# A hybrid decoder step on one core: paged-cache gathers of eight head dimensions instead of four, with single convolution buffers

## The chip, the core and the metric

The kernel runs on one core of one Trainium2 chip. The metric is the device time of one execution in microseconds. Three runs of the kernel before gave 2805.02, 2815.38 and 2817.81 us, so the median is 2815.38 us.

## What is computed

One layer of an autoregressive decoder, in float32, on 512 prompt tokens and, beside them, on one new token for each of 8 decode sequences. The 520 columns go through the same weights together.

```python
proj = rms_norm(x) @ w_in                 # 2048 -> 7168 + 16
# group A: stick-breaking attention, 8 heads of 128
z  = q.k * SCALE + logit_bias
lb = log_sigmoid(z); l1 = where(valid, lb - z, 0)
a  = where(valid, exp(lb + reverse_cumsum(l1) - l1), 0)
o_sb = rms_norm(a @ v)
# the decode tokens read 2048 cached positions each:
k_past = cache_sb_k[page_table]           # 8 sequences x 16 pages x 128 positions
v_past = cache_sb_v[page_table]
# group B: gated DeltaNet, 8 heads; causal conv of width 4 + SiLU on q, k, v
# then: output projection, residual, gated MLP with a causal conv of width 3,
# a per-layer input gate, final norm
```

## The kernel before, in words

The program is one stream for one core. TensorE does products of 128-row weight tiles with the 520 activation columns, each product as three matmuls on a high and a low part of both operands. A weight tile arrives in `w` by an SP DMA (L238, 512 KB for a half product of eight 128-row blocks), ScalarE casts it to `wh` (L242), and VectorE subtracts to get `wl` (L243). `w` and `wh` have two buffers each, `wl` three (`WB`). One product of `w_in` is two such halves, 96 matmuls of 128x260.

The order of the products is: the per-layer input projection, queries of heads 0 to 3, the eight key convolutions of group B, then four times query, key and value of group A (heads 0 to 3, with the queries of heads 4 to 7), then for the eight heads of group B the q convolution, the v convolution and the gate, then key and value of heads 4 to 7, then the output projection in two parts, and the MLP, whose weights go through a Strassen scheme (`strassen`, `block_product`). Between the products small chains (`sb_chain`, `gdn_chain`, `k_chain`) are advanced step by step by a hand-kept clock (`tick`).

The attention of the decode tokens is laid beside that stream. `decode_k` and `decode_v` read the cache page by page through `gather` (L406 to L411): for one group of four heads and one set of `DC` = 4 head dimensions, four indirect DMAs on the POOL queue, each of 128 rows of `DC` x 128 positions (2 KB a row, 256 KB a gather), fill one `kv` tile of 1 MB. There are two such tiles (`bufs=2`), so a gather for the tile after next waits until VectorE has read the tile before it. VectorE then does `DC` operations of 128x512 on the tile: L436 for keys, L466 for values. With `NDC` = 32 tiles for each of keys and values and two groups of heads there are 128 tiles, 512 gathers and 512 VectorE operations.

The order of instructions on each engine is fixed ahead of time by a planner: it takes ready instructions by priority, with its own estimate of how long each takes. `later(LATE)` puts the decode work last in priority, so it is placed wherever the planner expects an engine to be free and the data to be there. On the chip each engine then works strictly in that order.

```python
def gather(src, g, dc):                                             # L406
    t = dpool.tile([P, 4, DC * PAGE], F32, name="kv", bufs=2)
    for pg in range(4):
        G.indirect_dma_start(out=t[:, pg], out_offset=None, in_=src, in_offset=...)
```

`delta_decode` (L966 to L1044) is the recurrent part for the decode tokens. It needs the q, k and v convolutions of all eight heads. It loads the state in four tiles of 1 MB (`state`, L1000), which take turns in the same two `kv` buffers, and works on each in two pieces of 128x1024: a product (L1014), a reduction (L1016) and an addition (L1018), for two vectors. The value gathers of the second head group stand behind it, but for the first `VSPLIT` = 2 tiles.

`conv` (L594 to L612) copies a finished product to `cb` (ScalarE, L601, L602), writes three zero columns (POOL, L598), scales into `y` (ScalarE, L609) and adds three shifted terms (VectorE, L611 three times). `gdn_conv` then applies SiLU (L625, L626). `cb` and `y` of group B have two buffers each, from the pool `gdn`.

Other parts that the change touches: the tiles `q` and `kT` of an attention head (`sb_head`, two buffers each), the scan in `decode_k` (its result in a tile of its own, L445), the loads `mx` and `xr` ahead of the output projection (L1086, L1101), and the first weights of the MLP: before, a row sum of two weight blocks (`row_sum(0)`, an SP load and an accumulating POOL DMA) is started ahead of `strassen`, and the first block `a11` is loaded to a tile of the pool `wst`.

Of the kernel before, what the change touches and what calls it, by code (L numbers as in the profile page):

```python
# [16 lines left out]
P = 128  # L17
# [14 lines left out]
NPAGE = PAST // PAGE  # L32
DC = 4
NDC = HD // DC
# [6 lines left out]
AFTER = 2  # L41
MXB = 7
KK = 9.0
# [42 lines left out]
def program(tc, i, o):  # L86
# [143 lines left out]
    evacs = []  # L230
    last_wl = [None]
    last_w = [None]

    def weights(src, n, cols=P, after=None, eng=None, pool=None):
        w = wp.tile([P, 8, P], F32, name="w", bufs=WB[0])[:, :n, :cols]
        wh = (pool or wp).tile([P, 8, P], F32R, name="wh", bufs=4 if pool else WB[1])[:, :n, :cols]
        wl = wp.tile([P, 8, P], F32R, name="wl", bufs=WB[2])[:, :n, :cols]
        last_w[0] = nc.sync.dma_start(w, src).ins  # L238
        with contextlib.ExitStack() as st:
            if after is not None:  # L240
                st.enter_context(tc.issue_after(after))
            S.copy(wh, w)  # L242
        last_wl[0] = (eng or V).tensor_tensor(wl, w, wh.bitcast(F32), op=ALU.subtract).ins  # L243
        return wh, wl
# [144 lines left out]
    dpool = pool("dec", 1, "right")  # L389
    gdnp = pool("gdn", 2, "right")  # L390
    tp = gdnp
# [26 lines left out]
    def decode_k(g):  # L418
        with later(-EARLY):
# [6 lines left out]
            S.copy(qd, pq[:, :P])  # L426
        a2 = [dpool.tile([P, 4, PAGE], F32, name=f"dacc{j}") for j in range(2)]
        for dc in range(NDC):
# [15 lines left out]
        V.scalar_tensor_tensor(t1, s, 0.0, t1, op0=ALU.max, op1=ALU.add)  # L444
        inc = dpool.tile([P, 8 * PAGE], F32, name="inc", tag="junk")[:, :T]  # L445
        V.tensor_tensor_scan(inc, t1, zero.broadcast_to([P, T]), 0.0, op0=ALU.add, op1=ALU.add)
        pc = pstd("pc")
        PE.matmul(pc[:, :1], lhsT=C("carry"), rhs=inc[:, T - 1:T], start=True, stop=True)
        nb = dpool.tile([P, 1], F32, name="nb")
        V.tensor_scalar(nb, pc[:, :1], -1.0, None, op0=ALU.mult)  # L450
        V.tensor_tensor(s, s, inc, op=ALU.subtract)
        S.activation(s, s, AF.Exp, bias=nb)
# [4 lines left out]
    def decode_v(g, lo=0, hi=NDC):  # L457
# [3 lines left out]
        for dc in range(lo, hi):  # L461
            with later(LATE):
                vt = gather(i["cv"], g, dc)
                for d in range(DC):
                    junk = n4(dpool.tile([P, 8 * PAGE], F32, name="junk")[:, :4 * PAGE])
                    V.scalar_tensor_tensor(junk, vt[:, :, d], 1.0, A, op0=ALU.mult, op1=ALU.mult,  # L466
                                           accum_out=ov[:, dc * DC + d:dc * DC + d + 1])
# [307 lines left out]
    def sb_head(h):  # L775
        until("sb", ("z", h - 1))
        qT = sbp.tile([P, T], F32, name="q", bufs=2)
        nc.sync.dma_start(qT, qd_[h])
        ps = w_in(H + h)
        kT = sbp.tile([P, T], F32, name="kT", bufs=2)  # L780
        evac_nat(ps, kT, ks[:, h])
# [62 lines left out]
    for h in range(4):  # L844
        queries(4 + h, w_in(4 + h), sbp.tile([P, T], F32, name="q", bufs=2))
        sb_head(h)
# [119 lines left out]
    def delta_decode():  # L966
# [8 lines left out]
        V.tensor_tensor(cf[:, 0:2], cf[:, 0:2], sq, op=ALU.mult)  # L975
        rep = dpool.tile([P, 8 * PAGE], F32, name="rep", tag="junk")[:, :3 * P].rearrange("p (a r c) -> p a r c", a=3, r=2)
        V.tensor_copy(rep, cf.unsqueeze(2).broadcast_to([P, 3, 2, 64]))
# [22 lines left out]
        def state(c):  # L1000
            t = dpool.tile([P, 2, 1024], F32, name="st", tag="kv", bufs=2)
            nc.sync.dma_start(t.rearrange("p a c -> p (a c)"), i["rec"][:, c * 2048:c * 2048 + 2048])
            return t

        sqk = dpool.tile([P, 2, 64], F32, name="sqk")
        with later(LATE):
            for c in range(4):
                t = state(c)
                for a in range(2):
                    ch = c * 2 + a  # L1010
                    s3 = t[:, a].rearrange("p (k v) -> p k v", v=64)
                    for w, vecp in enumerate((qp, kp)):
                        tmp = dpool.tile([P, 8 * PAGE], F32, name="gtmp", tag="junk").rearrange("p (k v) -> p k v", k=16)
                        V.tensor_tensor(tmp, s3, vecp[:, 16 * ch:16 * ch + 16].unsqueeze(2).broadcast_to([P, 16, 64]), op=ALU.mult)  # L1014
                        part = sqk[:, w] if ch == 0 else dpool.tile([P, 64], F32, name="dpart")
# [45 lines left out]
    for h in range(4, H):  # L1061
        sb_head(h)
        if h == SBC:
            drain("gdn0", "gdn1")
            close(n=2)
            fpool = pool("res", 1)
            mpool = pool("mix", 1)
            NRES = 9
# [9 lines left out]
    for part in range(2):  # L1078
# [17 lines left out]
        for m in range(KC):  # L1096
# [3 lines left out]
            else:  # L1100
                xr = tp.tile([P, 544], F32, name="xr", tag="yg")[:, :TOK]  # L1101
                nc.sync.dma_start(xr, i["x"][m])
# [65 lines left out]
    close("right")  # L1168
    close(n=2)
    sp_ = pool("wst", 1)  # L1170
# [36 lines left out]

    row_sums = [row_sum(0)]

    def strassen(m, f, c1, c2):  # L1210
        src1, src2 = i["w_gate"][m], i["w_up"][m]
        b, a, c, d = [mp.tile([P, 512], F32, name=n)[:, 0:HALF] for n in ("pb", "pa", "pc", "pd")]
        a11 = raw(src1[:, :NP], "a11", sp_, 2)
        a12 = raw(src1[:, NP:], "w", wp, WB[0])
        s1 = row_sums.pop()
        p1, u2, u3 = [tp.tile([P, HALF], F32, name=n) for n in ("p1", "u2", "u3")]
# [265 lines left out]
```

## Time and profile before

| | |
|---|---|
| median of three runs | 2815.38 us (2805.02 to 2817.81) |
| the profiled execution, its own time | 2811.4 us |
| span of its trace | 2809.6 us |
| mean granted TensorE clock | 0.979 of full speed |
| TensorE busy | 2654.4 us, 94% of the span |
| VectorE busy | 1900.8 us, 68% |
| GpSimd (POOL) busy | 713.9 us, 25%, most of it before 1210 us |

A trace row names the line, the engine, what it writes and what it reads. "Idle before" is the time in which the engine had nothing running ahead of that instruction, and the releaser is what ended it. The chain of waits is followed back from the last instruction: at each step to what released it, or to the instruction ahead of it on its engine. TensorE's granted clock is 1.00 at 2.4 GHz; the other level is 1.2 GHz, so a mean of 0.95 over a stretch is a tenth of it at the lower level.

### The profile page before, as it was taken

How to read it: one execution, taken by the hardware profiler on the slowest of the kernel's cores; microseconds unless marked ns; L12 is line 12 of the kernel's file. 1: busy time of each engine (PE TensorE's matmuls, PEld its weight loads, DVE VectorE, ACT ScalarE, POOL GpSimd, SP SyncE). 2: the span in 40 equal slices, each digit the busy share in tenths (PEclk: the TensorE clock that was granted, in tenths of full speed). 3: DMA queues.
4: the chain of work that ended last, by engine and by line, in shares of the span. 5: the costliest groups of instructions: out<-in, count | busy, mean ns of one | idle time of the engine just before them, and what ended most of it. 6: DMA issues, size and time to landing. Idle time of an engine off the chain costs nothing.

```text
span 2809.6 us, 52566 instructions
## 1 busy us (share of the span) xinstructions
PE 2654.4 (94%) x21329; PEld 2593.8 (92%) x21329; DVE 1900.8 (68%) x3060; ACT 1159.0 (41%) x1936; POOL 713.9 (25%) x773
## 2 busy tenths in 40 slices
PE   8898899998999898979999999999998999999997
PEld 7898788998998788979999999999998999999997
DVE  7487767677779766677878888888885342433545
ACT  5454444333345541554444444444451131323433
POOL 4565556656650566210000000000000000000000
PEclk9999999999999999989999999999999999999998
DMA  5678778767775778675655555555556453433333
GB/s 189 225 251 257 231 225 265 239 213 230 241 240 151 251 235 264 178 214 159 180 155 177 166 178 165 175 168 175 168 163 226 137 155 93 139 95 94 110 114 114
DMA packets 194083, 519.99 MB, mean 185 GB/s; under 512 B 41712, under 2 KB 51824, under 8 KB 193328
## 3 DMA queue, kind: packets, MB, share of 16 engines
q1 hardware_dynamic: 138672, 336.13, 37.4%
q0 software_dynamic: 55168, 180.50, 21.9%
q8 instruction: 167, 2.74, 0.4%
q14 instruction: 76, 0.62, 0.1%
HBM read 463.05 MB, written 49.76 MB: 183 GB/s over the span
## 4 chain that ended last, share of the span: by engine, by line
PE 55%; DMA 16%; DVE 11%; POOL 8%; issue 8%; ACT 2%; DVEq 0%; POOLq 0%; SPq 0%; ACTq 0%
PE mm L264 25%; PE pb L1198 13%; PE pc L1198 8%; POOL kv L409 8%; DMA kv<-in_ck,idx 6%; DMA kv<-in_cv,idx 6%; PE pa L1198 4%; PE pd L1198 4%; DVE dacc L436 2%; DMA acc<-sqt 1%; DVE wl L243 1%; DVE junk L466 1%; DMA out_recs<-st 1%; DVE yg L611 1%; DVE dpart L1016 1%
## 5 line engine op out<-in xcount | busy, mean ns | idle before, releaser
L264 PE MATMUL mm<-ah,wl 128*128 128x260 f32 x4128 | 856.8, 288 | 30.6 <-DVE wl L243 30.4
L264 PE MATMUL mm<-ah,wh 128*128 128x260 f32 x4128 | 860.9, 289 | 17.6 <-ACT wh L242 12.5
L264 PE MATMUL mm<-al,wh 128*128 128x260 f32 x4128 | 854.4, 288 | 3.8 <-DVE al L374 3.3
L264 PEld LDWEIGHTS mm<-ah,wl 128*128 128x128 f32 x4128 | 649.3, 192 | 40.9 <-DVE wl L243 37.3
L264 PEld LDWEIGHTS mm<-ah,wh 128*128 128x128 f32 x4128 | 651.0, 192 | 25.0 <-ACT wh L242 13.5
L264 PEld LDWEIGHTS mm<-al,wh 128*128 128x128 f32 x4128 | 649.0, 192 | 8.8 <-DVE al L374 4.3
L242 ACT CAST wh<-w 128x1024 fp32r<-128x1024 f32 (+4 forms) x289 | 279.7, 968 | 654.7 <-PE mm L264 575.0
L243 DVE TENSOR_TENSOR wl<-w,wh 128x1024 fp32r<-128x1024 f32 (+4 forms) x282 | 315.7, 1120 | 228.4 <-ACT wh L242 223.2
L409 POOL DMA_INDIRECT kv<-in_cv,idx x256 | 283.5, 1107 | 259.0 <-DVE seed L867 74.2
L409 POOL DMA_INDIRECT kv<-in_ck,idx x256 | 293.3, 1146 | 187.0 <-DVE dacc L436 77.9
L1193 ACT CAST wh<-a 128x1024 fp32r<-128x1024 f32 x172 | 181.0, 1052 | 365.4 <-PE pc L1198 188.1
L466 DVE SCALAR_TENSOR_TENSOR junk<-kv,dacc 128x512 f32<-128x512 f32 x256 | 176.9, 691 | 110.0 <-DMA kv<-in_cv,idx 106.3
L436 DVE SCALAR_TENSOR_TENSOR dacc<-kv,qd,dacc 128x512 f32<-128x512 f32 x252 | 178.4, 747 | 101.0 <-DMA kv<-in_ck,idx 101.0
L1194 DVE TENSOR_TENSOR wl<-a,wh 128x1024 fp32r<-128x1024 f32 x172 | 210.1, 1221 | 43.3 <-ACT wh L1193 43.0
L1198 PE MATMUL pb<-ah,wh 128*128 128x260 f32 x774 | 220.7, 285 | 11.5 <-ACT wh L1193 11.5
L1198 PE MATMUL pb<-ah,wl 128*128 128x260 f32 x774 | 221.7, 286 | 5.6 <-DVE wl L1194 5.5
L1198 PE MATMUL pb<-al,wh 128*128 128x260 f32 x774 | 220.2, 284 | 0.0
L1357 POOL TENSOR_TENSOR y<-h,fr 128x260 f32<-128x260 f32 x8 | 6.9, 887 | 689.2 <-DVE fr L1352 689.2
L1198 PEld LDWEIGHTS pb<-ah,wh 128*128 128x128 f32 x774 | 147.3, 190 | 12.0 <-ACT wh L1193 12.0
L1198 PEld LDWEIGHTS pb<-ah,wl 128*128 128x128 f32 x774 | 147.7, 191 | 7.6 <-DVE wl L1194 7.5
L1198 PEld LDWEIGHTS pb<-al,wh 128*128 128x128 f32 x774 | 147.5, 191 | 0.0
L598 POOL MEMSET cbf<- 128x2 f32 x43 | 4.6, 107 | 543.5 <-DVE yf L611 543.3
(437 smaller groups left out, 4735.2 us busy)
## 6 DMA issues: line engine op xcount, KB each, us to landing
w<-in_w_in SPq DMA_DIRECT2D x112, 512.0 KB
a<-in_w_up SPq DMA_DIRECT2D x86, 512.0 KB
w<-in_w_down SPq DMA_DIRECT2D x48, 512.0 KB
w<-in_w_gate SPq DMA_DIRECT2D x43, 512.0 KB
s<-in_w_up SPq DMA_DIRECT2D x43, 512.0 KB
a<-in_w_gate SPq DMA_DIRECT2D x43, 512.0 KB
s<-in_w_up POOLq DMA_DIRECT2D x43, 512.0 KB, 7.7
w<-in_w_pg SPq DMA_DIRECT2D x32, 512.0 KB
```

Source lines behind the costliest of these rows:

```text
L242: S.copy(wh, w)
L243: last_wl[0] = (eng or V).tensor_tensor(wl, w, wh.bitcast(F32), op=ALU.subtract).ins
L264: last_mm[0] = PE.matmul(ps[:, hf, 0:HALF], lhsT=a, rhs=b[:, hf * HALF:(hf + 1) * HALF], start=(first and n == 0), stop=(last and n == 2)).ins
L409: G.indirect_dma_start(out=t[:, pg], out_offset=None, in_=src, in_offset=bass.IndirectOffsetOnAxis(ap=idx[:, g, dc, pg:pg + 1], axis=0))
L436: V.scalar_tensor_tensor(a2[dd % 2], kt[:, :, d], qd[:, dd:dd + 1], a2[dd % 2], op0=ALU.mult, op1=ALU.add)
L466: V.scalar_tensor_tensor(junk, vt[:, :, d], 1.0, A, op0=ALU.mult, op1=ALU.mult, accum_out=ov[:, dc * DC + d:dc * DC + d + 1])
L611: V.scalar_tensor_tensor(y, cb[:, j:j + L], cw[:, j:j + 1], y, op0=ALU.mult, op1=ALU.add)
L1016: V.tensor_reduce(part, tmp.rearrange("p k v -> p v k"), axis=AX.X, op=ALU.add)
L1193: S.copy(wh, w)
L1194: V.tensor_tensor(wl, w, wh.bitcast(F32), op=ALU.subtract)
L1198: last_mm[0] = PE.matmul(ps, lhsT=a[:, k], rhs=b, start=(start and k + n == 0), stop=(k == NP - 1 and n == 2), skip_group_check=not start).ins
L1357: e.tensor_tensor(y[:, j], hres[m + j][:, c], r, op=ALU.mult)
```

## The change

The gathers take eight dimensions at once, so a row is 4 KB, a gather 512 KB and a tile 2 MB; there are 64 tiles and 256 gathers, and still two tiles in the ring. The number and shape of the VectorE operations on the tiles (L436, L466) stay. The state of `delta_decode` comes in two tiles of two 1 MB loads each, worked on in 16 pieces of 128x512 instead of 8 of 128x1024. Besides, `cb` and `y` of group B, `q` and `kT` get one buffer each; `wl` two until the MLP, with every third one of the first four weight tiles in another pool; the second key accumulator shares its place with `junk`; the scan works in place; `mx` loads get six buffers instead of seven; the `xr` loads alternate between two pools with one buffer each. For the MLP the weight pool is opened again with three `wl`, its first block `a11` goes through the `w` ring, and the first row sum is started inside `strassen`, behind the loads of `a11` and `a12`.

```diff
-DC = 4
+DC = 8
-MXB = 7
+MXB = 6
...
+    WL = [2]
+    third = [0]
...
-        wl = wp.tile([P, 8, P], F32R, name="wl", bufs=WB[2])[:, :n, :cols]
+        third[0] = (third[0] + 1) % 3
+        own = pool if pool and third[0] == 0 else wp
+        wl = own.tile([P, 8, P], F32R, name="wl", bufs=WL[0] if own is wp else 1)[:, :n, :cols]
...
-    gdnp = pool("gdn", 2, "right")
+    gdnp = pool("gdn", 1, "right")
...
-        a2 = [dpool.tile([P, 4, PAGE], F32, name=f"dacc{j}") for j in range(2)]
+        a2 = [dpool.tile([P, 4, PAGE], F32, name=f"dacc{j}", tag=("dacc", "junk")[j]) for j in range(2)]
...
-        inc = dpool.tile([P, 8 * PAGE], F32, name="inc", tag="junk")[:, :T]
-        V.tensor_tensor_scan(inc, t1, zero.broadcast_to([P, T]), 0.0, op0=ALU.add, op1=ALU.add)
+        V.tensor_tensor_scan(t1, t1, zero.broadcast_to([P, T]), 0.0, op0=ALU.add, op1=ALU.add)
...
-        qT = sbp.tile([P, T], F32, name="q", bufs=2)
+        qT = sbp.tile([P, T], F32, name="q")
...
-        kT = sbp.tile([P, T], F32, name="kT", bufs=2)
+        kT = sbp.tile([P, T], F32, name="kT")
...
-            t = dpool.tile([P, 2, 1024], F32, name="st", tag="kv", bufs=2)
-            nc.sync.dma_start(t.rearrange("p a c -> p (a c)"), i["rec"][:, c * 2048:c * 2048 + 2048])
+            t = dpool.tile([P, 2, 2048], F32, name="st", tag="kv", bufs=2)
+            for a in range(2):
+                nc.sync.dma_start(t[:, a], i["rec"][:, c * 4096 + a * 2048:c * 4096 + a * 2048 + 2048])
...
-            for c in range(4):
-                t = state(c)
-                for a in range(2):
-                    ch = c * 2 + a
-                    s3 = t[:, a].rearrange("p (k v) -> p k v", v=64)
+            for c in range(2):
+                t = state(c).rearrange("p a c -> p (a c)")
+                for a in range(8):
+                    ch = c * 8 + a
+                    s3 = t[:, 512 * a:512 * a + 512].rearrange("p (k v) -> p k v", v=64)
...
+            xpool = pool("xres", 1)
...
-                xr = tp.tile([P, 544], F32, name="xr", tag="yg")[:, :TOK]
+                xr = (xpool.tile([P, TOK], F32, name="xr") if m % 2 else tp.tile([P, 544], F32, name="xr", tag="yg")[:, :TOK])
...
-    close(n=2)
+    close(n=4)
+    wp = pool("wts2", 1)
+    WL[0] = WB[2]
...
-    row_sums = [row_sum(0)]
+    row_sums = []
...
-        a11 = raw(src1[:, :NP], "a11", sp_, 2)
+        a11 = raw(src1[:, :NP], "a11", sp_, 2) if m else raw(src1[:, :NP], "w", wp, WB[0])
         a12 = raw(src1[:, NP:], "w", wp, WB[0])
-        s1 = row_sums.pop()
+        s1 = row_sums.pop() if m else row_sum(0)
```

## Rows read from the trace of the kernel before

**Rows 1.** The page, block 1: busy us of each engine over the span, its share of the span and its instructions.

```profile
PE 2654.4 (94%) x21329; PEld 2593.8 (92%) x21329; DVE 1900.8 (68%) x3060; ACT 1159.0 (41%) x1936; POOL 713.9 (25%) x773
```

**Rows 2.** Busy time of each engine by stretches of the span, in us from its start: length, busy us and instructions of each engine, granted clock, DMA share, GB/s. Gathers run in the first, second, third and fifth of them; the sixth is the start of the MLP, the seventh a long stretch of products with no gathers.

```profile
100.00:350.00 250.00, 225.74 (x1691) 214.35 (x1690) 187.06 (x385) 114.03 (x208) 148.49 (x136) 0.95 0.75 237
350.00:590.00 240.00, 223.66 (x1813) 209.40 (x1813) 171.07 (x417) 98.07 (x168) 144.87 (x135) 0.96 0.76 238
590.00:840.00 250.00, 227.42 (x1817) 224.01 (x1816) 187.20 (x360) 93.46 (x219) 154.25 (x143) 0.96 0.72 233
840.00:923.00 83.00, 77.35 (x574) 70.80 (x573) 78.52 (x132) 40.70 (x79) 8.16 (x7) 1.00 0.51 147
923.00:1130.00 207.00, 184.26 (x1339) 171.82 (x1338) 141.75 (x338) 83.19 (x125) 121.08 (x114) 0.96 0.78 257
...
1200.00:1250.00 50.00, 36.47 (x258) 35.09 (x257) 34.60 (x49) 23.26 (x35) 6.52 (x9) 0.83 0.75 217
...
2185.00:2740.00 555.00, 555.00 (x4629) 554.88 (x4628) 216.32 (x256) 165.61 (x205) 0.00 (x0) 1.00 0.37 115
```

**Rows 3.** The chain of waits: shares by line over the whole span (first row), and in the stretch from 600 to 700 us (second row).

```profile
PE mm L264 25%; PE pb L1198 13%; PE pc L1198 8%; POOL kv L409 8%; DMA kv<-in_ck,idx 6%; DMA kv<-in_cv,idx 6%; PE pa L1198 4%; PE pd L1198 4%; DVE dacc L436 2%; DMA acc<-sqt 1%; DVE wl L243 1%; DVE junk L466 1%; DMA out_recs<-st 1%; DVE yg L611 1%; DVE dpart L1016 1%
...
by line: DMA kv<-in_ck,idx 33.5%; POOL kv L409 29.9%; issue 20.5%; DVE dacc L436 9.0%; DVE yg L611 5.1%; DVE wl L243 1.1%; DVE zt L957 0.7%; ACT gv L625 0.6%; ACT gq L625 0.6%; DVEq L436 0.2%; ACT cbg L606 0.2%; ACT cs L626 0.2%; POOLq L409
```

**Rows 4.** Who waited for whom over the span: us in total, times, longest us.

```profile
DVE junk L466 <- DMA kv<-in_cv,idx: 106.3, 44, 5.4
DVE dacc L436 <- DMA kv<-in_ck,idx: 101.0, 43, 6.0
...
POOL kv L409 <- DVE dacc L436: 85.4, 26, 14.3
...
POOL kv L409 <- DVE junk L466: 74.1, 31, 6.8
```

**Rows 5.** The gathers (L409): duration in ns (least, median, most), the time from issue to landing, and two gathers in a row on POOL, with the idle time ahead of each.

```profile
L409 POOL DMA_INDIRECT kv<-in_ck,idx x256: 940/960/3297, 81.5 to 811.5; - x128
...
DMA to landing us min/median/max: 3.3/4.9/8.5
...
675.79 0.95 POOL L409 DMA_INDIRECT kv<-in_ck,idx  x1 [1.35 <-DVE dacc L436]
677.04 0.95 POOL L409 DMA_INDIRECT kv<-in_ck,idx  x1 [0.30 <-issue]
```

**Rows 6.** The VectorE operations on the gathered tiles: busy us in all, mean ns of one, idle before.

```profile
L436 DVE SCALAR_TENSOR_TENSOR dacc<-kv,qd,dacc 128x512 f32<-128x512 f32 x252 | 178.4, 747 | 101.0 <-DMA kv<-in_ck,idx 101.0
L466 DVE SCALAR_TENSOR_TENSOR junk<-kv,dacc 128x512 f32<-128x512 f32 x256 | 176.9, 691 | 110.0 <-DMA kv<-in_cv,idx 106.3 <-ACT dacc L452 0.2
```

**Rows 7.** Another DMA that POOL issues, of 512 KB: duration on POOL in ns (least, median, most), and from the page's list of DMA issues its size and the median us from issue to landing.

```profile
L1205 POOL DMA_DIRECT2D s<-in_w_up x43: 866/872/1252, 1210.3 to 2043.7; - x43
...
s<-in_w_up POOLq DMA_DIRECT2D x43, 512.0 KB, 7.7
```

**Rows 8.** ScalarE in order of time, three places in the key convolutions: the evacuation of a product to `cbg` (L601) stands ahead of the SiLU of the convolution before it (L625), which waits for that one's last L611. The last number in brackets is ScalarE's idle time.

```profile
165.56 0.58 ACT L601 COPY cbg<-mm 128x512 f32<-128x512 f32 x1
168.86 0.63 ACT L625 ACTIVATE gk<-yg 128x512 f32<-128x512 f32 x1 [1.35 <-DVE yg L611]
...
180.26 0.57 ACT L601 COPY cbg<-mm 128x512 f32<-128x512 f32 x1
182.15 0.63 ACT L625 ACTIVATE gk<-yg 128x512 f32<-128x512 f32 x1
...
221.65 0.58 ACT L601 COPY cbg<-mm 128x512 f32<-128x512 f32 x1
224.74 0.63 ACT L625 ACTIVATE gk<-yg 128x512 f32<-128x512 f32 x1 [1.13 <-DVE yg L611]
```

**Rows 9.** The work of `delta_decode` on the state, and a product of 128x512 from elsewhere (L1053): duration in ns, first and last start.

```profile
L1014 DVE TENSOR_TENSOR gtmp<-st,qkv x16: 1211/1218/1225, 850.7 to 917.0; 128x1024 f32<-128x1024 f32 x16
...
L1016 DVE TENSOR_REDUCE dpart<-gtmp x14: 1903/1982/2010, 860.8 to 919.5; 128x64 f32<-128x1024 f32 x14
...
L1018 DVE TENSOR_TENSOR sqk<-sqk,dpart x14: 208/216/225, 863.5 to 921.7; 128x64 f32<-128x64 f32 x14
...
L1053 DVE TENSOR_TENSOR up<-kvg,kvg x16: 684/691/694, 2122.3 to 2179.9; 128x512 f32<-128x512 f32 x16
```

**Rows 10.** The cast `wh` (L242): what ended ScalarE's idle time ahead of it, in us and times; and the subtractions `wl` (L243) on VectorE from 100 to 350 us and from 350 to 1130 us (count, busy us, mean ns, idle before).

```profile
  PE mm L264: 575.0, 166
...
  DMA w<-in_w_in: 8.8, 4
...
L243 DVE TENSOR_TENSOR wl<-w,wh 128x1024 fp32r<-128x1024 f32 x31 | 37.8, 1219 | 6.3 <-ACT wh L242 6.3
...
L243 DVE TENSOR_TENSOR wl<-w,wh 128x1024 fp32r<-128x1024 f32 (+1 forms) x100 | 114.5, 1145 | 7.0 <-ACT wh L242 6.7
```

**Rows 11.** The start of the MLP: TensorE's first matmul there with its idle time, and pieces of the chain of waits (start, us, what).

```profile
1212.53 0.59 PE L1198 MATMUL pb<-ah,wh 128*128 128x260 f32 x1 [10.79 <-ACT wh L1193]
...
1200.38 8.79 DMA acc<-sqt
...
1210.30 10.76 DMA s<-in_w_up
...
1224.83 4.38 PE pb L1198 x22
```

More of the change, by code (lines that the diff above doesn't have):

```diff
@@ L444, in decode_k @@
         V.scalar_tensor_tensor(t1, s, 0.0, t1, op0=ALU.max, op1=ALU.add)
-        inc = dpool.tile([P, 8 * PAGE], F32, name="inc", tag="junk")[:, :T]
-        V.tensor_tensor_scan(inc, t1, zero.broadcast_to([P, T]), 0.0, op0=ALU.add, op1=ALU.add)
+        V.tensor_tensor_scan(t1, t1, zero.broadcast_to([P, T]), 0.0, op0=ALU.add, op1=ALU.add)
         pc = pstd("pc")
-        PE.matmul(pc[:, :1], lhsT=C("carry"), rhs=inc[:, T - 1:T], start=True, stop=True)
+        PE.matmul(pc[:, :1], lhsT=C("carry"), rhs=t1[:, T - 1:T], start=True, stop=True)
         nb = dpool.tile([P, 1], F32, name="nb")
         V.tensor_scalar(nb, pc[:, :1], -1.0, None, op0=ALU.mult)
-        V.tensor_tensor(s, s, inc, op=ALU.subtract)
+        V.tensor_tensor(s, s, t1, op=ALU.subtract)
         S.activation(s, s, AF.Exp, bias=nb)
@@ L464, in decode_v @@
                 for d in range(DC):
-                    junk = n4(dpool.tile([P, 8 * PAGE], F32, name="junk")[:, :4 * PAGE])
+                    junk = n4(dpool.tile([P, 4 * PAGE], F32, name="junk"))
                     V.scalar_tensor_tensor(junk, vt[:, :, d], 1.0, A, op0=ALU.mult, op1=ALU.mult,
@@ L844, in program @@
     for h in range(4):
-        queries(4 + h, w_in(4 + h), sbp.tile([P, T], F32, name="q", bufs=2))
+        queries(4 + h, w_in(4 + h), sbp.tile([P, T], F32, name="q"))
         sb_head(h)
@@ L975, in delta_decode @@
         V.tensor_tensor(cf[:, 0:2], cf[:, 0:2], sq, op=ALU.mult)
-        rep = dpool.tile([P, 8 * PAGE], F32, name="rep", tag="junk")[:, :3 * P].rearrange("p (a r c) -> p a r c", a=3, r=2)
+        rep = dpool.tile([P, 4 * PAGE], F32, name="rep", tag="junk")[:, :3 * P].rearrange("p (a r c) -> p a r c", a=3, r=2)
         V.tensor_copy(rep, cf.unsqueeze(2).broadcast_to([P, 3, 2, 64]))
@@ L1006, in delta_decode @@
         with later(LATE):
-            for c in range(4):
-                t = state(c)
-                for a in range(2):
-                    ch = c * 2 + a
-                    s3 = t[:, a].rearrange("p (k v) -> p k v", v=64)
+            for c in range(2):
[3 more added lines that the diff above has]
+                    s3 = t[:, 512 * a:512 * a + 512].rearrange("p (k v) -> p k v", v=64)
                     for w, vecp in enumerate((qp, kp)):
-                        tmp = dpool.tile([P, 8 * PAGE], F32, name="gtmp", tag="junk").rearrange("p (k v) -> p k v", k=16)
-                        V.tensor_tensor(tmp, s3, vecp[:, 16 * ch:16 * ch + 16].unsqueeze(2).broadcast_to([P, 16, 64]), op=ALU.mult)
+                        tmp = dpool.tile([P, 4 * PAGE], F32, name="gtmp", tag="junk").rearrange("p (k v) -> p k v", k=8)
+                        V.tensor_tensor(tmp, s3, vecp[:, 8 * ch:8 * ch + 8].unsqueeze(2).broadcast_to([P, 8, 64]), op=ALU.mult)
                         part = sqk[:, w] if ch == 0 else dpool.tile([P, 64], F32, name="dpart")
```

## The prediction

> **What bounds the kernel now.** I read the busy times first. TensorE is busy 94% of the span [rows 1], which leaves 155 us; the question is where they lie, so the table by stretches comes next [rows 2]. In the long run of products with no gathers (2185 to 2740) TensorE has no idle time at all. In the four stretches with gathers, 947 us long, it stands idle for 24.3 + 16.3 + 22.6 + 22.7 = 85.9 us, and its granted clock is 0.95 to 0.96 instead of 1.00. A mean of 0.95 over 250 us costs 12.5 us of full-speed time; the four make 12.5 + 9.6 + 10.0 + 8.3 = 40.4 us. So the stretches with gathers hold about 126 us that better-fed products would not need: the ceiling of any gain from the decode work.
>
> The chain of waits says why [rows 3]. Over the whole span the gathers' issue on POOL and their landing hold 20% of it, some 560 us, though the decode work is meant to be filler. In a stretch of 100 us (600 to 700) nearly all of it is one loop: landing 33.5%, issue on POOL 29.9%, gaps between issues within 20.5%, VectorE's use of the tile 9.0%. The list of waits shows both sides of that loop [rows 4]: VectorE stands 207 us for gathered tiles (87 waits, 2.4 us each), POOL 160 us for VectorE to give a tile back. While VectorE stands for a tile, everything behind it in its fixed order stands too: the `wl` subtractions, the convolution terms and the small chains that TensorE needs.
>
> The loop can be added up. A gather costs POOL 0.95 us and 0.30 us of gap [rows 5], so four cost 5.0 us; the last lands 4.9 us after its issue; four VectorE operations take 4 x 0.75 = 3.0 us [rows 6]. One tile's round is 12.9 us, and with two tiles in the ring a tile of 1 MB goes by every 6.45 us at best. In the last stretch 114 gathers pass in 207 us [rows 2], which is 7.3 us per tile. The ring runs within 13% of its own limit: it is the bound there, and TensorE's idle time follows from it.
>
> **The change, part by part.** *Gathers.* A gather of eight dimensions has as many rows (128), each twice as long. The trace of before has no such gather. Its price on POOL lies between today's 0.95 us (price by rows) and 1.9 us (price by bytes); I take 0.95, because POOL spends 0.87 us on a plain DMA of 512 KB [rows 7], no more than on a gather of half that size. Its landing lies between 4.9 us, as today, and 9.8 us, twice that; I take the 7.7 us of that other DMA of 512 KB [rows 7]. A round is then 5.0 + 7.7 + 8 x 0.75 = 18.7 us, with two tiles 9.35 us per 2 MB or 4.7 us per MB: 27% under the 6.45 of now. POOL's 512 issues become 256, which takes some 320 us off its queue; the convolutions' memsets, which share that queue, find it freer. VectorE's own work on the tiles is the same.
>
> So the ring stops being the bound, and what binds next is VectorE's order and TensorE itself. How much of the 126 us comes back? Nothing if the waits for tiles only become rarer and longer; all of it if decode hides entirely. The stretch from 840 to 923 is the nearest row: there VectorE is still loaded (78.5 of 83 us) but only seven gathers are issued, and TensorE idles 5.65 us, 6.8%, at a clock of 1.00 [rows 2]. At that rate the 947 us would lose 64 us instead of 126. I take **-62 us**, with the ends 0 and -126.
>
> *Single `cb` and `y`.* The evacuation of the next product must now wait for the last L611 of the convolution before. Where that is earlier anyway it costs nothing. In three places of the key convolutions the evacuation came first, by 3.3, 1.9 and 3.1 us [rows 8]; elsewhere the two mostly stand a microsecond or more apart in the right order. TensorE itself has a second product tile to go on with; what suffers is ScalarE's queue, where the `wh` casts stand behind the waiting copy, and POOL's, where gathers stand behind the waiting memset. Between 0 and 8 us by those three; I take **+6 us**, nearer the upper end, because these queues now wait for each other.
>
> *`delta_decode`.* Sixteen products of 1.22 us become 32 of 0.69 us [rows 9], +2.6 us; sixteen additions more, 16 x 0.21 = +3.4 us; 32 reductions of half the length cost at least half of 1.98 us each, and perhaps 0.1 us more, +0 to +2 us. VectorE is nearly full in that stretch [rows 2], so it lies on the path: **+7 us** (6 to 8). The four SP loads of 1 MB stay four.
>
> *Start of the MLP.* TensorE idles 10.8 us there for its first block [rows 11], which the change loads earlier. But the chain runs through POOL: the accumulations into `acc`, then the row sum's accumulating DMA, issued at 1210.3 and 10.8 us long, then the third product at 1224.8. It still does, so an earlier first product only waits later, for the row sum: **0**, between -11 and +5 us (the sum's SP load now stands behind two others).
>
> *At nothing:* `wl` with two buffers, since `wh` has two as well and the cast waits for TensorE anyway (575 us of ScalarE's idle time) [rows 10], so a third `wl` could not be filled earlier; without that cover it costs two matmuls, 0.24 us, per half product. `q` and `kT` with one: their next write is a whole product away (96 x 0.12 = 11.5 us, from the run of products [rows 2]); if that cover goes, one 256 KB load per head, 8 x 5 us. Six `mx` buffers, the alternating `xr` and the scan in place: hidden by the output projection's products, or the same VectorE work.
>
> *Weights beside larger gathers.* In the whole run the cast waited 8.8 us for a `w_in` load, in 4 places [rows 10], with gathers running beside most of them: nothing to charge. The Trainium skill, "DMA: Bandwidth & Descriptors", section "Queues, rings and completion order", says that each DMA engine goes round the queues that have work, a whole packet at a time; by that, rows twice as long would give the gathers a larger turn against the weights. By the row the term is 0; by that rule the sum would be that of the last rival below. No run here shows yet which.
>
> The sum is made against the profiled execution, 2811.4 us, which stands 4.0 us under the median of 2815.4: 2811.4 - 62 + 6 + 7 + 0 = **2762 us**.
>
> **The rivals.** *The waits only grow rarer and longer.* The planner puts a tile's first operation where it expects the landing. On the chip it came 2.4 us later, 87 times [rows 4]. If a tile of 2 MB comes twice as late, half as often, VectorE still stands 207 us and TensorE gets nothing back: 2811.4 + 13 = 2824 us, no change that can be told. For it: a transfer twice as long errs twice as much. Against: half of the loop is issue, not transfer [rows 3], and the longest wait now is 6.0 us.
>
> *Single convolution buffers become the bound* (the slower side). If all 24 convolutions run into their predecessor by the longest overlap of now, 3.3 us [rows 8], and ScalarE's delay reaches TensorE through the casts, 24 x 3.3 = 79 us in place of 6: 2835 us. It decides once a convolution, from its evacuation to its last L611, outlasts a product, 11.5 us. For it: the 3.3 us case, where filler operations stood between its terms. Against: shorter waits of VectorE shorten that very span.
>
> *Weights come late.* If each of the 131 half products in that part [rows 10] gets its `w` 0.6 us too late, 79 us more than the forecast: 2841 us. Against it stands the 8.8 us.
>
> *The change does not do what it says:* a gather costs POOL 1.9 us. A round is then 8.8 + 7.7 + 6.0 = 22.5 us, 5.6 us per MB, still 13% under now; about half of the gain is lost, 2793 us. It counts with the forecast.
>
> **How the numbers follow.** About 0.5%, 14 us, is what a measurement of this kernel can tell from no change; faster is thus below 2801, slower above 2829. Forecast, ring no longer the bound, also at half its gain: 0.69. Rarer and longer waits: 0.17. Convolution buffers: 0.09. Late weights: 0.05. So faster 0.69, same 0.17, slower 0.14. The forecast's own range is 2697 (the whole 126 us back, 2811 - 126 + 12) to 2800. The range for 8 in 10 takes in the first rival and leaves out both slower ones and the last bit at the lower end: 2700 to 2828.
>
> **What would show it.** Right: 256 gathers of about 1 us on POOL; gathers and their landings well under 20% of the chain; VectorE's waits for `kv` under 130 us; TensorE's idle time in the decode part under 70 us and its clock there at 0.97 or more; the stretch from the first gather to the MLP shorter by 40 to 70 us, and nothing of note after it. Wrong: waits for `kv` still about 200 us with single ones above 8 us (first rival); L601 or the memset waiting for L611 in most convolutions (second); `wh` waiting for `w_in` loads (third); gathers of 1.9 us on POOL (fourth).

## The result: 3.1% faster, 37 us below the predicted time

The changed kernel takes 2725.57 us (median, 2722.24 to 2728.86) where the one before takes 2815.02 us in the same runs: a ratio of 0.969, 95% interval 0.966 to 0.972, or -89.5 us. The prediction said -53 us and 2762 us; the time lies inside its range. The profiled execution took 2726.1 us, with a span of 2724.2.

First the page of the changed kernel: the busy times (answers to [rows 1]) and the chain of waits by line (to [rows 3]).

```profile
PE 2623.6 (96%) x21329; PEld 2574.0 (94%) x21329; DVE 1909.6 (70%) x3108; ACT 1159.2 (43%) x1935; POOL 434.1 (16%) x517
...
PE mm L268 33%; PE pb L1205 13%; PE pc L1205 9%; PE pa L1205 4%; PE pd L1205 4%; DMA kv<-in_ck,idx 3%; POOL kv L413 3%; DVE dacc L440 2%; DMA kv<-in_cv,idx 2%; DVE wl L247 1%; DVE junk L469 1%; DMA w<-in_w_in 1%; DMA out_recs<-st 1%; DVE yg
```

The gathers' issue (L413) and landing hold 8% of the chain instead of 20%, and POOL lost 280 us of work. To see where the 85 us of span went, both spans are cut at the same piece of work, the third product of the MLP (8470 matmuls come before it in either kernel). Columns as in [rows 2]; the changed kernel first, then the one before.

```profile
0.00:1143.64 1143.64, 1072.15 (x8470) 1028.07 (x8470) 900.62 (x1863) 533.93 (x977) 362.65 (x383) 0.98 0.74 246
...
1143.64:2724.20 1580.56, 1551.46 (x12860) 1545.90 (x12860) 1009.02 (x1246) 625.25 (x958) 71.48 (x134) 0.99 0.50 151
```

```profile
0.00:1224.83 1224.83, 1102.73 (x8470) 1048.64 (x8470) 891.67 (x1814) 533.01 (x979) 642.42 (x639) 0.96 0.73 230
...
1224.83:2809.60 1584.77, 1551.70 (x12860) 1545.19 (x12860) 1009.15 (x1247) 626.01 (x959) 71.45 (x134) 0.99 0.50 150
```

Ahead of the cut 81.2 us are gone; behind it 4.2. Of the 81.2, TensorE's idle time gives 50.6 (1224.83 - 1102.73 = 122.1, now 71.5), and 30.6 come from the same matmuls taking less time, at a granted clock of 0.98 instead of 0.96.

The waits say what ended the idle time (us in total, times, longest; VectorE's and POOL's answer to [rows 4], ScalarE's to [rows 10]).

```profile
DVE dacc L440 <- DMA kv<-in_ck,idx: 43.2, 14, 7.3
DVE junk L469 <- DMA kv<-in_cv,idx: 30.1, 13, 6.2
...
POOL kv L413 <- DVE junk L469: 131.8, 24, 15.2
POOL kv L413 <- DVE dacc L440: 119.5, 20, 14.5
...
POOL cbg L601 <- DVE yg L614: 92.4, 9, 28.0
...
ACT wh L246 <- DMA w<-in_w_in: 36.3, 8, 7.9
```

VectorE stands 73 us for gathered tiles, 27 times, instead of 207 us, 87 times. A single wait is hardly longer (2.7 us against 2.4). In its list of waits POOL now waits 251 us for VectorE's operations on the tiles (L440, L469) instead of 160: the ring's slack has changed sides. The gathers themselves (answers to [rows 5]):

```profile
L413 POOL DMA_INDIRECT kv<-in_ck,idx x128: 933/1020/3259, 82.7 to 683.2; - x128
L413 POOL DMA_INDIRECT kv<-in_cv,idx x128: 932/996/2392, 287.2 to 1012.7; - x128
DMA to landing us min/median/max: 4.1/7.0/12.2
```

Before, the value gathers had

```profile
L409 POOL DMA_INDIRECT kv<-in_cv,idx x256: 940/948/2547, 334.1 to 1119.3; - x128
```

Twice the bytes cost POOL 5 to 6% more by the median, and land 2.1 us later. The start of the MLP has the same chain as in [rows 11], pieces of the chain in order of time:

```profile
1118.62 8.01 DMA acc<-sqt
...
1128.56 10.75 DMA s<-in_w_up
...
1143.64 5.13 PE pb L1205 x22
```

And the convolutions' evacuations (L604) now stand right behind the SiLU of the one before (L628), instead of ahead of it as in [rows 8]:

```profile
148.50 0.63 ACT L628 ACTIVATE gk<-yg 128x512 f32<-128x512 f32 x1 [0.72 <-DVE yg L614]
149.15 0.57 ACT L604 COPY cbg<-mm 128x512 f32<-128x512 f32 x1
...
162.00 0.63 ACT L628 ACTIVATE gk<-yg 128x512 f32<-128x512 f32 x1 [1.05 <-DVE yg L614]
162.65 0.57 ACT L604 COPY cbg<-mm 128x512 f32<-128x512 f32 x1
```

### The profile page after: what moved, and what is told of

It reads as the page before. It is cut to its first block, busy times and chain, and to the rows that moved or that the text cites. A ratio compares the mean times of both kernels' runs of the same rounds, so it can differ in the third digit from the quotient of the medians.

```text
span 2724.2 us, 52117 instructions
## 1 busy us (share of the span) xinstructions
PE 2623.6 (96%) x21329; PEld 2574.0 (94%) x21329; DVE 1909.6 (70%) x3108; ACT 1159.2 (43%) x1935; POOL 434.1 (16%) x517
## 4 chain that ended last, share of the span: by engine, by line
PE 65%; DMA 11%; DVE 11%; issue 6%; POOL 3%; ACT 3%; SPq 0%; DVEq 0%; POOLq 0%; ACTq 0%
PE mm L268 33%; PE pb L1205 13%; PE pc L1205 9%; PE pa L1205 4%; PE pd L1205 4%; DMA kv<-in_ck,idx 3%; POOL kv L413 3%; DVE dacc L440 2%; DMA kv<-in_cv,idx 2%; DVE wl L247 1%; DVE junk L469 1%; DMA w<-in_w_in 1%; DMA out_recs<-st 1%; DVE yg L614 1%; DMA st<-in_rec 1%
## 5 line engine op out<-in xcount | busy, mean ns | idle before, releaser
L268 PE MATMUL mm<-ah,wl 128*128 128x260 f32 x4128 | 845.1, 285 | 23.8 <-DVE wl L247 23.7
L268 PEld LDWEIGHTS mm<-ah,wl 128*128 128x128 f32 x4128 | 642.6, 190 | 30.8 <-DVE wl L247 27.4
L268 PEld LDWEIGHTS mm<-ah,wh 128*128 128x128 f32 x4128 | 644.2, 190 | 15.2 <-ACT wh L246 7.5
L268 PEld LDWEIGHTS mm<-al,wh 128*128 128x128 f32 x4128 | 642.4, 190 | 7.1 <-DVE al L378 4.4
L440 DVE SCALAR_TENSOR_TENSOR dacc<-kv,qd,dacc 128x512 f32<-128x512 f32 x252 | 178.6, 743 | 43.3 <-DMA kv<-in_ck,idx 43.2
L469 DVE SCALAR_TENSOR_TENSOR junk<-kv,dacc 128x512 f32<-128x512 f32 x256 | 176.1, 688 | 35.2 <-DMA kv<-in_cv,idx 30.1
L413 POOL DMA_INDIRECT kv<-in_cv,idx x128 | 141.2, 1103 | 317.4 <-DVE junk L469 128.7
L413 POOL DMA_INDIRECT kv<-in_ck,idx x128 | 155.5, 1215 | 194.5 <-DVE dacc L440 119.5
L1205 PE MATMUL pc<-ah,wh 128*128 128x260 f32 x430 | 121.5, 283 | 5.9 <-ACT wh L1200 5.9
L1200 ACT CAST wh<-w 128x1024 fp32r<-128x1024 f32 x88 | 92.5, 1051 | 78.1 <-PE pd L1205 50.3
```

The source lines that it names most:

```text
L268: last_mm[0] = PE.matmul(ps[:, hf, 0:HALF], lhsT=a, rhs=b[:, hf * HALF:(hf + 1) * HALF], start=(first and n == 0), stop=(last and n == 2)).ins
L440: V.scalar_tensor_tensor(a2[dd % 2], kt[:, :, d], qd[:, dd:dd + 1], a2[dd % 2], op0=ALU.mult, op1=ALU.add)
L1205: last_mm[0] = PE.matmul(ps, lhsT=a[:, k], rhs=b, start=(start and k + n == 0), stop=(k == NP - 1 and n == 2), skip_group_check=not start).ins
```

## The experiments

Theory: the whole gain comes from the gathers, since the ring loop no longer bounds; the rest of the change costs little. Rivals: the gain comes from the freed buffers and the other small edits; the deeper ring alone (4 MB under way instead of 2) gives it; single convolution buffers cost time that larger gathers pay back. The runs were made on several occasions. The kernel before takes 2815 us on the first (the result) and on the last (experiment 6), and 2828 to 2838 us on the three between them, so ratios are compared, each to runs of before on the same occasion.

**1. All of the change but the larger gathers.** The changed kernel with four dimensions to a gather and the ring of two 1 MB tiles of before. The pieces of the edit that are not shown set `VSPLIT` and `AFTER` to 4 in place of 2, so that as many bytes of values are read early as after the change, and loop over the four tiles of the state.

```
-DC = 8
+DC = 4
-            t = dpool.tile([P, 2, 2048], F32, name="st", tag="kv", bufs=2)
+            t = dpool.tile([P, 2048], F32, name="st", tag="kv", bufs=2)
```

> Everything as after the change, but tiles of 1 MB gathered by four dimensions (512 gathers), ring of two, state in four tiles as before. If the gain comes from the decode loop (larger tiles or fewer issues), it goes away: 2795 to 2820 us, waits of VectorE for tiles back near 200 us. If it comes from the rest of the change (convolution buffers, pieces of 512, start of the MLP, other places of the weight tiles), the time stays at 2725 to 2745 us.

Measured: 2831.5 us, ratio 0.998 (0.996 to 1.001). VectorE's waits for the tiles:

```profile
DVE junk L469 <- DMA kv<-in_cv,idx: 81.8, 36, 6.0
DVE dacc L440 <- DMA kv<-in_ck,idx: 70.7, 33, 6.1
```

69 waits and 152 us are back, and so is the time. The small edits together are worth nothing that can be measured; the gain hangs on the size of gathers and tiles.

**2. Single convolution buffers alone**, in the kernel before:

```
-    gdnp = pool("gdn", 2, "right")
+    gdnp = pool("gdn", 1, "right")
```

> As before the change, with one buffer each for the convolution's two tiles (and with them one for the xr loads and the last mx loads). The prediction's term says +6 us: 2815 to 2825 us. The rival that convolutions bind says 2880 us or more. If the planner only puts the next evacuation behind the SiLU and nobody waits for it, it is within 5 us of before: 2810 to 2820 us.

Measured: 2831.0 us, ratio 0.996 (0.993 to 0.999). They cost nothing. In the changed kernel the planner puts the evacuations behind the SiLUs, as the lines above show.

**3. How much the gathers still hold back.** One of four pages is gathered and read four times.

```
-        for pg in range(4):
+        for pg in range(1):
```

> As after the change, but only one of the four pages of a tile is gathered and VectorE reads it four times over (the attention of the decode tokens is computed from a quarter of the cache): the same VectorE operations, 64 gathers, a quarter of the traffic. If the waits for tiles and the late weight loads that are left after the change (73 us and 36 us in its trace) still hold TensorE, the time falls to 2680 to 2705 us. If what is left is VectorE's own work and its order, it stays within 10 us: 2715 to 2730 us.

Measured: 2684.4 us, ratio 0.945 (0.942 to 0.948), with TensorE busy 97%:

```profile
PE 2611.9 (97%) x21329; PEld 2563.2 (96%) x21329; DVE 1911.2 (71%) x3108; ACT 1168.6 (44%) x1942; POOL 218.8 (8%) x325
```

So the changed kernel still loses to its gathers: 2725.6 - 2684.4 = 41 us, or 1.6 to 2.4 points of the ratio (it has 0.961 and 0.969 on two occasions).

**4. The deeper ring with gathers of the old size.** Tiles of 2 MB, each page in two gathers of 256 KB (512 gathers):

```
-            G.indirect_dma_start(out=t[:, pg], out_offset=None, in_=src,
+            for j in range(DC // GD):
+                G.indirect_dma_start(out=t[:, pg, j * GD * PAGE:(j + 1) * GD * PAGE], out_offset=None, in_=src,
```

> As after the change, tiles of 2 MB in a ring of two, but each page comes in two gathers of four dimensions: 512 gathers of 256 KB. If the issue on POOL is what counted, most of the gain goes: 2780 to 2810 us. If what counted is that the ring holds twice as much, it stays: by the loop's sum a round is 8 x 1.25 + 4.9 + 6.0 = 20.9 us, 10.4 us per 2 MB against 9.4 after and 12.9 before, so 2725 to 2750 us.

Measured: 2919.7 us, ratio 1.027 (1.021 to 1.034), far from all that was expected. So it was run again on another chip, beside the changed kernel as a yardstick, and with four tiles of 1 MB in place of two of 2 MB (`DC = 4`, `bufs=4`):

> The same kernel as e2_split_gathers (tiles of 2 MB, 512 gathers of 256 KB) beside the kernel after on one chip. If its slowness belongs to the gathers' number, it is again slower than before (1.02 or more) and TensorE again has some 90 us of idle time without a releaser, all of it while gathers run. If it was that one chip or hour, it falls to 0.98 to 1.00 and that idle time goes.

> The kernel after the change, unaltered, on the chip of the runs of this call: the yardstick for them. 0.966 to 0.972 of before, and no idle time of TensorE without a releaser.

> As after the change, but four tiles of 1 MB gathered by four dimensions: the ring holds the same 4 MB as after, with 512 gathers of 256 KB. If the depth of the ring is what pays, it is near after: 0.965 to 0.98 of before. If the number of gathers is what costs, it is no faster than before: 0.99 to 1.03.

Measured: split gathers 2916.4 us, 1.028 (1.024 to 1.032); the changed kernel 2725.7 us, 0.961 (0.958 to 0.964); four small tiles 2925.1 us, 1.030 (1.025 to 1.036). So it is not one chip, and not the size of the tile. With the same tiles and the same ring, on one occasion, the larger gathers are 191 us faster than the small ones. VectorE's waits for tiles are nearly gone in the four-tile kernel (2.4 us), yet it is slower than before. TensorE has another kind of idle time instead, with no releaser ("issue"). Its waits in the two kernels, split gathers first:

```profile
PE mm L270 <- issue: 77.2, 126, 1.8
PE pr L226 <- issue: 12.1, 8, 3.7
```

```profile
PE mm L268 <- issue: 79.2, 127, 2.3
PE pr L224 <- issue: 17.8, 7, 8.0
```

In order of time it looks so, TensorE in the four-tile kernel:

```profile
298.48 0.49 PE L268 MATMUL mm<-ah,wh 128*128 128x260 f32 x2 [0.70 <-issue]
298.80 0.28 PE L268 MATMUL mm<-al,wh 128*128 128x260 f32 x1
299.89 0.28 PE L268 MATMUL mm<-al,wh 128*128 128x260 f32 x1 [0.81 <-issue]
300.01 0.40 PE L268 MATMUL mm<-ah,wl 128*128 128x260 f32 x2
300.25 0.28 PE L268 MATMUL mm<-ah,wh 128*128 128x260 f32 x1
301.32 0.38 PE L268 MATMUL mm<-ah,wh 128*128 128x260 f32 x1 [0.80 <-issue]
301.50 0.43 PE L268 MATMUL mm<-al,wh 128*128 128x260 f32 x1
302.77 0.38 PE L268 MATMUL mm<-al,wh 128*128 128x260 f32 x1 [0.84 <-issue]
302.95 0.43 PE L268 MATMUL mm<-ah,wl 128*128 128x260 f32 x1
```

TensorE goes on in steps of 1.4 us, two to four matmuls each. ScalarE's casts are late in the same kernel too: 108.6 us of waits, 18 of them, end by a releaser that the profile does not name. All such idle time of TensorE together is 114 us here, and the granted clock of the whole run is 0.954. The changed kernel beside it has 7.1 us, where none was expected, and 0.986. On the first occasion the profiles showed 1.5 us for the changed kernel and 1.8 us, with a clock of 0.979, for the one before. The loop sum, which promised a gain for these kernels, knows no such term.

**5. What brings these stalls.** Three kernels, all from the four-tile one: rows of 512 bytes, a quarter of the traffic; POOL waits for the tile two before to land, so that 8 gathers at most are under way instead of 16; three tiles.

```
-            G.indirect_dma_start(out=t[:, pg], out_offset=None, in_=src,
+            G.indirect_dma_start(out=t[:, pg, :PAGE], out_offset=None, in_=src.rearrange("n (d t) -> (n d) t", d=DC),
```

```
+        if len(ring) >= 2:
+            land = dpool.tile([P, 4, 1], F32, name="land")
+            G.tensor_copy(land, ring[-2][:, :, 0:1])
```

```
-        t = dpool.tile([P, 4, DC * PAGE], F32, name="kv", bufs=4)
+        t = dpool.tile([P, 4, DC * PAGE], F32, name="kv", bufs=3)
```

> The kernel with four 1 MB tiles and 512 gathers, with one edit: each gather brings rows of 512 bytes instead of 2 KB (one of its four dimensions, which is then read four times; three quarters of the cache are left out). The number of gathers, of rows and of buffers stays. Theory 'bytes': what slowed the four-tile kernel to 1.03 of before is the traffic of 4 MB kept under way; with a quarter of it the time falls to that of the quarter-gather kernel or a little above, 2680 to 2730 (0.945 to 0.965 of before), TensorE's idle time with no releaser under 15 us. Theory 'rows': it is the number of gathers and rows under way (16 gathers, 2048 rows), whatever they carry; then TensorE still shows over 60 us of idle time with no releaser, its clock stays below 0.965, and the time is 2850 or more.

> The kernel with four 1 MB tiles and 512 gathers, with one edit: before the four gathers of a tile POOL copies one column of the tile two before it, so that it waits until those have landed; at most 8 gathers are under way instead of 16, as in the kernel before, but a tile need no longer be freed by VectorE at once. Theory 'rows under way': below a limit that lies between 8 and 16 gathers the stalls without a releaser are gone (under 15 us), and since the loop is now landing and issue alone, (4 x 1.25 + 4.9)/2 = 5.0 us per MB beside 6.45 of before, the time falls below before: 2725 to 2790, 0.96 to 0.985. Theory 'number of gathers': 512 issues on POOL hold the time wherever the ring stands, so 2810 to 2850 (0.995 to 1.005). Theory 'any deeper ring is bad': 2900 or more.

> Three 1 MB tiles and 512 gathers: at most 12 gathers under way, between the two-tile kernel (8, ratio 0.998) and the four-tile kernel (16, ratio 1.030). Theory 'rows under way' with a gradual cost: a time between, 2840 to 2900, idle time without a releaser between 11 and 79 us. With a threshold above 12: no such idle time (under 15 us) and a ring that waits less, 2760 to 2820. The loop sum alone (a third tile takes VectorE's share out of the round) gives 2760 to 2790 as well.

Measured: short rows 2885.3 us, 1.019 (1.017 to 1.021); eight in flight 2865.9 us, 1.015 (1.010 to 1.020); three tiles 2875.5 us, 1.017 (1.015 to 1.019). TensorE's first wait in each, in that order:

```profile
PE mm L268 <- issue: 62.4, 102, 2.6
```

```profile
PE mm L268 <- issue: 28.7, 42, 2.3
```

```profile
PE mm L268 <- issue: 47.3, 95, 1.6
```

With a quarter of the bytes most of the stalls remain (90 us in all), so it is not the traffic alone. The limit of eight halves them without ending them, to 55 us in all, while the two-tile kernel of experiment 1, which also has eight under way, shows 18 us: the number under way is not it alone. Three tiles (78 us) lie between two (18) and four (114): a gradual cost.

**6. Breaks between the gathers.** Counted from the trace of the four-tile kernel, some 110 to 130 of 138 stalls over 0.3 us, depending on what counts as a break, came where POOL had issued more than eight gathers without one. So POOL was given filler writes ahead of every second tile of the four-tile kernel.

```
+        if dc % 2 == 0:
+            for j in range(12):
+                G.memset(pause, float(j))
```

> The kernel with four 1 MB tiles and 512 gathers (1.030 of before), with one edit: ahead of every second tile POOL writes a small scratch tile twelve times, some 2.5 to 3 us, so that no more than 8 gathers of 256 KB are issued without a break; number, size and ring stay. Counted over five traces, TensorE's stalls without a releaser come at 0 to 5 in 100 us while the unbroken run of gathers is 8 or fewer, and at 10 to 43 in 100 us beyond that. Theory 'unbroken runs': with the runs cut at 8 those stalls fall from 120 us to under 40 us, the clock rises from 0.954 to 0.965 or more, and, although POOL has some 180 us more to do, the time falls to 2770 to 2860 (0.98 to 1.01 of before). Rival 'the number of gathers, or the deep ring as such': the stalls stay above 80 us and the time at 2890 or more (1.02 or more), the pauses coming on top.

Measured: 2834.8 us, ratio 1.007 (1.004 to 1.010), clock 0.977. TensorE's idle time without a releaser is 3.0 us in all, and its list of waits looks like that of before again:

```profile
PE mm L268 <- DVE wl L247: 33.2, 25, 4.3
PE mm L268 <- ACT wh L246: 24.9, 10, 4.9
```

So neither 512 gathers nor a ring of 4 MB must bring the stalls. But the breaks did not fall as meant. In some stretches twelve writes and more stand together, in others a single one parts the tiles, as here on POOL:

```profile
436.68 0.95 POOL L418 DMA_INDIRECT kv<-in_cv,idx  x1 [0.30 <-issue]
437.63 0.22 POOL L416 MEMSET pause<- 128x128 f32 x1
438.00 1.24 POOL L418 DMA_INDIRECT kv<-in_cv,idx  x1 [0.16 <-issue]
```

And behind 865 us there is no write left. From 908 to 1120 us POOL does 112 gathers and nothing else, with four waits of over a microsecond among them and up to 68 gathers between two of these (all the writes, then POOL in that stretch: busy us, instructions, granted clock, DMA share, GB/s):

```profile
L416 POOL MEMSET pause<- x768: 204/205/1033, 75.0 to 864.5; 128x128 f32 x192
...
908.00:1120.00 212.00, 124.59 (x112) 0.98 0.77 247
```

TensorE has no idle time without a releaser in it. The four-tile kernel also does 112 gathers and nothing else on POOL in its last stretch of gathers, and there TensorE stalls for 25 us:

```profile
963.00:1202.00 239.00, 122.33 (x112) 0.91 0.69 216
...
PE mm L268 <- issue: 22.1, 38, 1.7
```

No write stands among the gathers in either stretch, so here it is not the writes that took the stalls away, and long runs of gathers do not bring them by themselves: the theory of unbroken runs, whose numbers came true, does not hold. What else differs is the occasion. This run was made when the kernel before took 2814.9 us, as on the first occasion; all kernels that stall were run when it took 2828 to 2838. On those occasions the unaltered changed kernel has 7.1 us of such idle time instead of 1.5, and the kernel before with single convolution buffers 14.0 instead of 1.8; the kernel with a quarter of the gathers has none there, so the occasion alone does not bring it either. The four-tile kernel was not run on the last occasion, nor this one on another; what the writes did, and what differs between the occasions, stays open. All kernels side by side:

```
                      ratio   before, us   clock   TensorE idle, no releaser   VectorE waits for tiles
before                1       2815         0.979     1.8 us                    207 us
single conv buffers   0.996   2838         0.974    14                         155
two 1 MB tiles        0.998   2838         0.976    18                         152
with filler writes    1.007   2815         0.977     3                         116
eight under way       1.015   2828         0.966    55                          52
three 1 MB tiles      1.017   2828         0.962    78                          50
short rows            1.019   2828         0.960    90                          10
split gathers         1.028   2833         0.955   111                          72
four 1 MB tiles       1.030   2833         0.954   114                           2
changed (256)         0.969   2815         0.986     1.5                        73
changed, again        0.961   2833         0.986     7.1                        60
```

Among the kernels with 512 gathers on the three occasions with stalls, the stalls mostly grow as VectorE's waits shrink (split gathers, 72 and 111, do not fit), and nearly all come while gathers are issued. A stream of TensorE's own instructions that comes too slowly beside so many gathers would look like this. No row here shows it; the larger of the profile's two instruction queues takes the same share of the DMA engines' time in the kernel before and in the four-tile kernel:

```profile
q8 instruction: 167, 2.74, 0.4%
```

The cause stays open. On the last occasion the kernel with filler writes, nearly without stalls and with half of VectorE's waits gone, was still no faster than before; what a deeper ring of small gathers gives without stalls and without writes was not measured.

**7. More of the V gathers early** (`VSPLIT = 6` in place of 2 in the changed kernel).

> As after the change, but six instead of two value tiles of the second head group stand ahead of the recurrent decode part, in the stretch from about 700 to 840 us in which the trace of after shows almost no gathers and VectorE at 54 to 72%. If gathers crowded into what follows still cost there, it is 5 to 20 us faster than after (0.96 to 0.967 of before); if the state's loads and the convolution chain now wait behind the tiles, it is slower than after.

Measured: 2723.4 us, 0.961 (0.957 to 0.964), the same as the changed kernel beside it. Neither case of the expectation came: whether two or six V tiles are read early does not matter.

## Why the prediction was right, and where its sizes were off

- *What bounds the kernel: right.* With larger gathers VectorE's waits fell by 134 us, and TensorE's idle time and clock followed. In the stretch with gathers (100 to 1130 us before, 100 to 1030 after) the idle time of TensorE that VectorE ended fell from 61.8 to 28.5 us, and that which ScalarE ended from 27.7 to 6.8. That the loop alone held the time is not shown: no kernel made the loop faster with small gathers without something else in its way.
- *Price of a gather: right.* 1.00 to 1.02 us by the median where 0.95 was taken, not the 1.9 of the fourth rival; landing 7.0 us where 7.7 was taken.
- *The gathers' term, -62 us: too small, though its rate held.* It set 126 us of idle time and lost clock in 947 us against the 6.8% that the stretch from 840 to 923 loses, 64 us. Measured, 81.2 us came back ahead of the MLP. From 100 to 1030 us the changed kernel idles 42.7 us of 930:

```profile
100.00:1030.00 930.00, 887.35 (x7051) 848.71 (x7049) 764.87 (x1667) 424.63 (x791) 296.26 (x277) 0.98 0.75 254
```

  A clock of 0.98 over it costs another 0.02 x 930 = 18.6 us by the prediction's own reckoning, which makes 61 us, or 6.6%. What is left is thus as it was forecast; what was there to gain was larger. The same reckoning over all of 100 to 1130 us before gives 91.6 + 40.4 = 132 us, with the 5.65 us of 840 to 923 that the ceiling left out, so some 71 us came back here. The other 10 of the 81.2 lie outside this stretch and in matmuls that took less time than the granted clock alone explains; no run parts them. These are estimates, since the clock is read to two digits.
- *Single `cb` and `y`, +6 us: wrong, nothing.* In the kernel before they change the time by -0.4%. The memset does wait now (92 us on POOL, 9 times), but POOL has the time, and the evacuations moved behind the SiLUs.
- *`delta_decode`, +7 us: the work is there, the time is not.* VectorE's products take 21.8 us in 32 pieces, against 19.5 in 16 of [rows 9], the reductions 34.6 against 31.6, the additions 6.6 against 3.0: 9 us more, where 6 to 8 were taken. Yet without larger gathers the whole change measures 0.998, at most some 1 us slower by its interval. From 795 to 882 us, where it runs, VectorE is busy 99% of the time, more than the 95% of before, but TensorE is busy 84.5 of the 87 us, at full clock:

```profile
795.00:882.00 87.00, 84.45 (x628) 77.77 (x628) 86.10 (x174) 42.66 (x76) 4.87 (x6) 1.00 0.50 147
```

  TensorE loses 2.9% here, beside 6.8% before. A full engine puts its work on the path only if something waits for it in that stretch, and here almost nothing does.
- *Start of the MLP, 0: right.* The row sum's two transfers still end the wait, 10.75 us as in [rows 11].
- *Weights, 0: right in the sum, but not for the reason given.* The cast's waits for `w_in`, 8.8 us before, grew to 36.3 us. TensorE's waits for the split weights fell all the same, those for `wl` as follows (before, then after), those for `wh` from 17.3 to 11.3 us:

```profile
PE mm L264 <- DVE wl L243: 30.4, 27, 3.1
...
PE mm L268 <- DVE wl L247: 23.7, 14, 7.2
```

  The rule of the Trainium skill, "DMA: Bandwidth & Descriptors", section "Queues, rings and completion order", which the third rival rested on, points the way that the cast's waits went. The two other traces with 4 KB rows and all the gathers agree with it (31.4 and 38.9 us); the traces with 2 KB rows have 15 us at most, experiment 1 has 5.4. No run changes the length of the rows alone, and the price is far below the 79 us of that rival.
- *First rival, rarer and longer waits: refuted.* They became rarer, 87 to 27, and only 0.3 us longer in the mean.

Of the signs named for being right all came (256 gathers of about 1 us, 8% of the chain, 73 us of waits, 42.7 us of idle time, a clock of 0.98) but one: the part ahead of the MLP became 81 us shorter, not 40 to 70.

In numbers: the forecast's -62 + 13 = -49 us of span stands against -85.4 measured. If the costs that did not show are taken as nothing, 19 of the 36 us that it missed are the gathers' term ahead of the MLP, 13 are those costs, and 4 lie behind the MLP's start. All three err to the same side, so the time, though inside the range, lies near its lower end.

## What to carry to other kernels

Where a gather costs its issuing engine the same for 2 KB rows as for 4 KB, ask for more bytes with each: here that gave 3 to 4%, and no ring with the small gathers gave anything. An edit that seems to take an effect away shows nothing until the kernel with the effect has been run beside it: the filler writes looked like the cure of the stalls, and the stalls were as absent where no write stood. A loop that is shown to bind may be summed from its rows, but a sum over one loop does not see what a faster loop does to other engines: the same sum promised a gain for the deeper ring, which came out 3% slower. Buffers that only the planner's order needs can be given up if that order can move.

## What the runs showed of the hardware

- A gather's price on POOL hardly depends on its bytes: medians of 948 to 1020 ns for 64 KB (short rows), 256 KB (before) and 512 KB (changed) at 128 rows each. It is not fixed, though: in the run with 64 gathers of 512 KB the medians are 1210 and 1267 ns.
- TensorE can lose over 110 us, in the lines shown in steps of 1.4 us, with no releaser in the records, while another engine issues small gathers. The same number of gathers in a ring of the same size cost it 3 us on another occasion, and nothing there in a stretch of 112 gathers with no filler write among them. Neither bytes nor the number of gathers nor the size of the ring nor an unbroken run of gathers explains it alone.
- The granted clock went with TensorE's idle time: 0.986 with the changed kernel, 0.991 with a quarter of the gathers, 0.954 with four small tiles. In the changed kernel 30.6 of the 81.2 us came back as faster matmuls.
